# Every fourth weight unit: lo by a ScalarE copy and an accumulating DMA in place of a VectorE subtraction

## The chip, the cores and the metric

The kernel runs on one core of a Trainium2 chip. The time is device microseconds from launch to end. A profile is one execution recorded by the hardware profiler; its span goes from the first to the last instruction. Engines are called PE (TensorE, matmuls), PEld (its weight loads), DVE (VectorE), ACT (ScalarE), POOL (GpSimd) and SP (SyncE, which here only issues DMAs).

## The reference

A decoder trunk on 256 tokens of width 2048, float32, two layers. Layer 0 mixes tokens with an 8-head retention, layer 1 with sliding-window attention; each layer then has a SwiGLU of hidden width 5632 and a gated addition of a per-layer embedding. What matters here is that nearly all work is `h @ w` for large weights:

```
for i in range(DEPTH):
    h = rmsnorm(x, norm_mix[i])
    x = x + (retention_mixer(h, ret_w_in, ret_gn, ret_w_out) if i == 0
             else swa_mixer(h, swa_w_in, swa_sinks, swa_w_out))
    gate, up = split(rmsnorm(x, norm_ffn[i]) @ ffn_w_in[i], 2)
    x = x + (silu(gate) * up) @ ffn_w_out[i]
    x = x + sigmoid(rmsnorm(x, norm_ple[i]) @ ple_w_gate[i]) * (p[i] @ ple_w_proj[i])
return rmsnorm(x, norm_final)
```

The weights are read once each, 494 MB in all from HBM.

## The kernel before

TensorE multiplies in a shorter float32 form, float32r. To keep precision, every operand is split exactly into two parts: hi is the value rounded to float32r, lo is what is left over. A product is three matmuls: activation hi times weight hi (line 159), activation hi times weight lo (line 160), activation lo times weight hi (line 161).

The weights come in **units**: 256 rows by 512 columns, laid out as 128 partitions by 2 by 512, so 512 KB and one run of 4 KB in each partition. Eight units or more, over the whole contraction, make a **chunk**: 512 output columns for all 256 tokens, accumulated in two PSUM tiles. A unit takes 2 row blocks x 2 token tiles x 3 products = 12 matmuls. There are 928 units: 256 in the retention, 264 in each SwiGLU (8 a chunk going in, 22 a chunk going out), 36 in each embedding stage, 72 in attention.

`run` goes through all units in one order. At the step of unit i it issues the load of unit i + 5 (`LOADS`; SP, line 130, into one of five raw buffers), then the split of unit i + 3 (`AHEAD`; `split_weights`, into one of four hi and four lo buffers), then the twelve matmuls of unit i. With the last unit of a chunk its accumulators are evicted (`done`), and what follows from them (transposes on VectorE, splits of the new activations, scores, softmax) is put into `side`, a list of generators that are advanced by one step behind each unit. Each engine carries out its instructions in this program order, and a semaphore holds an instruction back until its operands are there and its target buffer is free.

The split of a weight unit is line 208, a ScalarE copy of raw into hi with rounding, and line 209, a VectorE subtraction raw - hi into lo. The raw buffer is free when both have read it; hi and lo are free when the unit's last matmuls have read them.

POOL computes only a few powers for the norms (lines 265, 360, 702) after its start.

Of the kernel before, what the change touches and what calls it, by code (L numbers as in the profile page):

```python
# [15 lines left out]
ALU = mybir.AluOpType  # L16
# [27 lines left out]
class Lhs:  # L44
    """A transposed activation, split exactly into two float32r parts."""

# [8 lines left out]
class Chunk:  # L55
    """512 output columns for all tokens, accumulated over the whole contraction, in pieces of
    a token tile and some of the columns."""

# [6 lines left out]
class Unit:  # L65
    """KU blocks of 128 rows of a weight, in one chunk's columns."""

    def __init__(self, chunk, src, kts, lhs):
        self.chunk, self.src, self.kts, self.lhs = chunk, src, kts, lhs
        self.w = None  # L70


class Stage:
    """A part of the trunk with tiles of its own, from its first unit to its last."""

# [3 lines left out]
    def linear(self, w, block, lhs, done, units=None, chunk=None):  # L79
        """One chunk: block of 512 columns of a weight laid out by `_units`."""  # L80
        ch = chunk or Chunk(self, done)
        for u in units if units is not None else range(w.shape[1]):
            self.units.append(Unit(ch, w[block, u], range(KU * u, KU * u + KU), lhs))
            ch.left += 1
# [3 lines left out]
def tile_trunk(ctx, tc, ins, out):  # L88
# [18 lines left out]

    # ---------------------------------------------------------------- streams
    side = deque()
# [23 lines left out]
    def split_weights(u):  # L133
        raw = u.w
        hi = whi.tile([P, KU, NW], F32R, name="hi")
        lo = wlo.tile([P, KU, NW], F32R, name="lo")
        for part in u.parts:
            split(hi[:, part, :], lo[:, part, :], raw[:, part, :])
        u.w = (hi, lo)

    def multiply(u, which, left):
        """The unit's products for some pieces of its chunk; `left` of the chunk's units are
        still to come."""
        ch = u.chunk
        need(u.lhs, u.kts)
        if ch.acc is None:
            ch.acc = []
            for n, (_, cols) in enumerate(ch.pieces):
                bank, name = (ps_acc, "acc") if n < NT else (ps_at, "at")
                ch.acc.append(bank.tile([P, NW], F32, name=name)[:, : cols.stop - cols.start])  # L150
        hi, lo = u.w
        for j, k in enumerate(u.kts):
            first = not ch.begun and j == 0
            last = left == 0 and j == KU - 1
            for n in which:
                t, cols = ch.pieces[n]
                sl = slice(t * P, (t + 1) * P)
                xh, xl = u.lhs.hi[:, k, sl], u.lhs.lo[:, k, sl]
                nc.tensor.matmul(ch.acc[n], xh, hi[:, j, cols], start=first, stop=False)  # L159
                nc.tensor.matmul(ch.acc[n], xh, lo[:, j, cols], start=False, stop=False)  # L160
                nc.tensor.matmul(ch.acc[n], xl, hi[:, j, cols], start=False, stop=last)  # L161

    def run(stages, begin):
        """All units in order, their weights AHEAD units ahead; between them, steps of side work.
        The products of the units that end the last chunk go piece by piece of its output."""
        units = [(st, u) for st in stages for u in st.units]
        for n, (_, u) in enumerate(units[:LOADS]):
            if n < AHEAD:
                next(begin)
            load(u, 1 if n else KU)  # L170
            if n < AHEAD:
                split_weights(u)
        side.append(begin)
        now = None
        pools = ExitStack()
        last = [u for _, u in units[-AHEAD - 1 :]]
        assert len({id(u.chunk) for u in last}) == 1
        for i, (st, u) in enumerate(units):
            if st is not now:
                pools.close()  # L180
                st.open_(st, pools)
                now = st
            if i + LOADS < len(units):
                load(units[i + LOADS][1])
            if i + AHEAD < len(units):
                split_weights(units[i + AHEAD][1])
            if u is last[0]:
                break
            ch = u.chunk
            ch.left -= 1  # L190
            multiply(u, range(len(ch.pieces)), ch.left)
            ch.begun = True
            if ch.left == 0:
                g = ch.done(ch.acc)
                if g is not None:
                    side.append(g)
            step_side()
        ch = last[0].chunk
        for n, (t, cols) in enumerate(ch.pieces):
            for i, u in enumerate(last):  # L200
                multiply(u, [n], len(last) - 1 - i)
            ch.done(ch.acc[n], t, cols)
        pools.close()

    # ------------------------------------------------------------ small pieces
    def split(hi, lo, src, scale=None):
# [9 lines left out]
    def transpose_pair(srcs):  # L216
        """Two [128, 128] blocks of both token tiles -> a PSUM tile [128, 2, S]."""
        tr = ps_tr.tile([P, 2, S], F32, name="tr")
# [5 lines left out]
    def transposes(dst, src):  # L224
        """Steps that transpose src [128, NT, 512] into dst [128, 4, S], by blocks of 32 x 32."""
        n = P // SQ
# [10 lines left out]
    def blocks(src, i):  # L237
        """Blocks 2i and 2i + 1 of 128 columns of both token tiles."""
        return [[src(t)[:, b * P : (b + 1) * P] for t in range(NT)] for b in (2 * i, 2 * i + 1)]

    class Norm:
        """Sums of squares of the residual's chunks, and the transposed residual times the gain.
        The scale by token, inv, is applied behind the product with the weights."""

# [22 lines left out]
        def places(self, c, src):  # L267
            """Steps that put a chunk's four transposed blocks in place."""
            for j in range(4):
# [8 lines left out]
    def residual(stage, norm, c):  # L278
        """A chunk of an output projection onto the residual, then the next norm's part."""

# [14 lines left out]

    # --------------------------------------------------------------- retention
    def retention(norm, next_norm, w_in, w_out):
# [97 lines left out]

    # ---------------------------------------------------- sliding-window attention
    def swa(norm, next_norm, w_in, w_out):
# [36 lines left out]
        def q_done_of(j):  # L434
            def q_done(acc):
# [12 lines left out]
                def scores(i):  # L448
                    """Of heads 2i and 2i + 1: the numerators and denominators' parts."""
                    ats = [ps_at.tile([P, 3 * P], F32, name="at") for _ in range(2)]  # L450
# [97 lines left out]
        for j in range(SKV):  # L548
            stage.linear(w_in, j, norm.lhs, q_done_of(j))
        # The first chunks' last units wait for the last group of heads.  # L550
        n = KD // KU
# [7 lines left out]

    # --------------------------------------------------------------------- FFN  # L560
    def ffn(layer, norm, next_norm):
# [57 lines left out]

    # --------------------------------------------------------------------- PLE  # L620
    def ple(layer, norm, next_norm, final):
# [12 lines left out]
        def pair(c):  # L634
# [3 lines left out]
            def gate_done(acc):  # L638
# [7 lines left out]
                def later():  # L646
                    # The last reads of the old operand are queued: its place is free.
                    for b, xt in enumerate(st["xt"]):
# [35 lines left out]
            def gate_last(acc, t, cols):  # L684
                """A piece of the last chunk; with a token tile's last one, its rows go out."""
                fin, rest, row = st["fin"], st["rest"], xs[:, t, :]
# [37 lines left out]

    # ------------------------------------------------------------------- trunk
    norms = [Norm(w, layer) for layer in range(DEPTH) for w in range(3)] + [Norm(None, 0)]
# [14 lines left out]
    def load_x():  # L741
        """The first norm's operand comes transposed, in step with the first chunk's weights."""
        for b in range(KD // KU):
# [19 lines left out]
def _constants():  # L763
    """Tables that follow from the shapes alone."""
    h = np.arange(RH, dtype=np.float64)
# [14 lines left out]
def _units(w):  # L780
    """[K, N] -> [N / 512, K / 256, 128, 2, 512]: each unit in one piece, by partitions."""
    k, n = w.shape
# [3 lines left out]
def _heads(w):  # L786
    """The retention's columns by heads: q and k, v, g."""
    q, k, v, g = np.split(w, [RH * RK, 2 * RH * RK, 2 * RH * RK + RH * RV], axis=1)
# [46 lines left out]
```

## Time and profile before

| | |
|---|---|
| time, median of 2 runs | 2649.66 us (2649.51 to 2649.82) |
| span of the profiled execution | 2647.9 us |
| runs less the span | 1.6 to 1.9 us |
| PE, PEld busy | 2629.2, 2142.7 us |
| DVE, ACT, POOL busy | 1817.2, 1223.7, 14.6 us |
| DMA | 497.79 MB, 188 GB/s |

The profiled execution's own time isn't given apart from its span; the runs lie 1.6 to 1.9 us above that.

How to read the lines: a group of instructions gives line, engine, operation, target<-sources, shapes and count, then busy time, the mean duration in ns of one, and after a second bar the idle time of the engine just before them with what ended it. A line of waits reads "who <- for whom: us in total, times, longest us". A line of the time line is start, duration, engine, line, operation, and in brackets the idle time before it and who ended it. A line of DMA issues ends with KB each and the median time from issue to landing. The chain of work is followed backwards from the last instruction, at each step to what released it.

### The profile page before, as it was taken

The page shows a single profiled execution, that of the slowest core. Times are in us where ns is not written, and L with a number is a line of the kernel's source. Part 1 is how long each engine was busy: PE and PEld are TensorE (multiplying, and loading weights), DVE is VectorE, ACT ScalarE, POOL GpSimd, SP SyncE. Part 2 cuts the span into 40 slices and gives each one's busy share as a digit, 9 for nine tenths or more (in the row PEclk, how much of TensorE's full clock was granted, in tenths as well). Part 3 has the DMA queues.
Part 4 walks back from the last instruction along what each step waited for, and adds up shares of the span by engine and source line. Part 5 has one row for each costly group of instructions (what it writes and reads, how often), then busy time and mean ns, then how long its engine had stood idle before and what let it go on. Part 6 is the DMA issues. An engine that isn't in the chain of part 4 may idle for free.

```text
span 2647.9 us, 31279 instructions
## 1 busy us (share of the span) xinstructions
PE 2629.2 (99%) x11632; PEld 2142.7 (81%) x11632; DVE 1817.2 (69%) x2567; ACT 1223.7 (46%) x1527; POOL 14.6 (1%) x30
## 2 busy tenths in 40 slices
PE   8999999999999999999999999999999999999998
PEld 6888888888888888888888887777888888888887
DVE  6777777766666667676555786888757575755565
ACT  6444444444444444444444555555444444444444
POOL 0000000000000000000000000000000000000000
PEclk9999999999999999999999999999999999999999
DMA  8555555565566565656655655346666666555564
GB/s 277 185 185 186 185 186 183 181 190 184 194 192 193 191 197 190 198 186 197 190 187 187 190 193 169 121 135 202 189 198 189 197 194 194 192 188 187 189 207 144
DMA packets 140506, 497.79 MB, mean 188 GB/s; under 512 B 15809, under 2 KB 19009, under 8 KB 140225
## 3 DMA queue, kind: packets, MB, share of 16 engines
q1 hardware_dynamic: 140064, 495.73, 58.5%
q8 instruction: 91, 1.49, 0.2%
q14 instruction: 63, 0.51, 0.1%
q10 hardware_dynamic: 288, 0.07, 0.0%
HBM read 493.63 MB, written 2.10 MB: 187 GB/s over the span
## 4 chain that ended last, share of the span: by engine, by line
PE 95%; DVE 3%; issue 1%; DMA 1%; ACT 0%; SPq 0%; ACTq 0%; POOLq 0%; POOL 0%; DVEq 0%
PE acc L159 31%; PE acc L161 31%; PE acc L160 31%; DVE lo L209 1%; DVE xt L233 1%; PE at L454 1%; PE tr L506 0%; PE at L532 0%; DMA raw<-in_ret_w_in 0%; PE at L323 0%; DVE xTl L212 0%; DVE qkT L233 0%; DMA xs<-in_x 0%; PE at L350 0%; PE at L352 0%
## 5 line engine op out<-in xcount | busy, mean ns | idle before, releaser
L209 DVE TENSOR_TENSOR lo<-raw,hi 128x1024 fp32r<-128x1024 f32 (+1 forms) x929 | 1131.8, 1221 | 720.2 <-ACT hi L208 712.8
L208 ACT ACTIVATE hi<-raw 128x1024 fp32r<-128x1024 f32 (+1 forms) x929 | 982.0, 1058 | 1210.9 <-PE acc L161 1117.4
L159 PE MATMUL acc<-hi,xTh 128*128 128x512 f32 x2592 | 1011.0, 390 | 6.6 <-ACT hi L208 5.4
L161 PE MATMUL acc<-hi,xTl 128*128 128x512 f32 x2592 | 1008.0, 389 | 0.8 <-DVE xTl L212 0.6
L160 PE MATMUL acc<-lo,xTh 128*128 128x512 f32 x2592 | 1008.7, 389 | 0.0
L159 PEld LDWEIGHTS acc<-hi,xTh 128*128 128x128 f32 x2592 | 487.3, 188 | 111.6 <-ACT hi L208 5.6
L161 PEld LDWEIGHTS acc<-hi,xTl 128*128 128x128 f32 x2592 | 487.0, 188 | 103.6 <-DVE xTl L212 2.5
L160 PEld LDWEIGHTS acc<-lo,xTh 128*128 128x128 f32 x2592 | 487.3, 188 | 100.5 <-issue 0.7
L161 PE MATMUL acc<-hi,hTl 128*128 128x512 f32 x704 | 278.4, 396 | 0.0
L160 PE MATMUL acc<-lo,hTh 128*128 128x512 f32 x704 | 278.4, 395 | 0.0
L159 PE MATMUL acc<-hi,hTh 128*128 128x512 f32 x704 | 278.4, 395 | 0.0
L233 DVE STREAM_TRANSPOSE xt<-h 32x256 f32<-32x256 f32 x352 | 153.6, 436 | 6.8
L161 PEld LDWEIGHTS acc<-hi,hTl 128*128 128x128 f32 x704 | 132.2, 188 | 32.1
L160 PEld LDWEIGHTS acc<-lo,hTh 128*128 128x128 f32 x704 | 132.2, 188 | 32.1
L159 PEld LDWEIGHTS acc<-hi,hTh 128*128 128x128 f32 x704 | 132.2, 188 | 31.9
L233 DVE STREAM_TRANSPOSE xt<-xs 32x256 f32<-32x256 f32 x320 | 139.5, 436 | 6.0
L161 PE MATMUL acc<-hi,yTl 128*128 128x512 f32 x256 | 101.2, 396 | 0.0
L160 PE MATMUL acc<-lo,yTh 128*128 128x512 f32 x256 | 101.2, 395 | 0.0
L159 PE MATMUL acc<-hi,yTh 128*128 128x512 f32 x256 | 101.2, 395 | 0.0
L233 DVE STREAM_TRANSPOSE qkT<-qk 32x256 f32<-32x256 f32 x128 | 55.8, 436 | 10.2 <-ACT qk L315 8.1
L211 ACT ACTIVATE xTh<-xt,gains 128x256 fp32r<-128x256 f32 x80 | 35.8, 499 | 56.0 <-DVE xt L233 51.6
L159 PEld LDWEIGHTS acc<-hi,yTh 128*128 128x128 f32 x256 | 48.1, 188 | 11.7
(124 smaller groups left out, 1178.2 us busy)
## 6 DMA issues: line engine op xcount, KB each, us to landing
raw<-in_ffn_w_in SPq DMA_DIRECT2D x352, 512.0 KB, 4.2
raw<-in_ret_w_in SPq DMA_DIRECT2D x191, 512.0 KB, 3.6
raw<-in_ffn_w_out SPq DMA_DIRECT2D x176, 512.0 KB, 4.0
raw<-in_ret_w_out SPq DMA_DIRECT2D x64, 512.0 KB, 4.0
raw<-in_ple_w_gate SPq DMA_DIRECT2D x64, 512.0 KB, 3.8
raw<-in_swa_w_in SPq DMA_DIRECT2D x40, 512.0 KB, 3.7
raw<-in_swa_w_out SPq DMA_DIRECT2D x32, 512.0 KB, 3.7
raw<-in_ple_w_proj SPq DMA_DIRECT2D x8, 512.0 KB, 4.0
```

Source lines behind the costliest of these rows:

```text
L159: nc.tensor.matmul(ch.acc[n], xh, hi[:, j, cols], start=first, stop=False)
L160: nc.tensor.matmul(ch.acc[n], xh, lo[:, j, cols], start=False, stop=False)
L161: nc.tensor.matmul(ch.acc[n], xl, hi[:, j, cols], start=False, stop=last)
L208: nc.scalar.activation(hi, src, AF.Copy)
L209: nc.vector.tensor_tensor(lo, src, hi.bitcast(F32), op=ALU.subtract)
L211: nc.scalar.activation(hi, src, AF.Copy, scale=scale)
L233: nc.vector.transpose(dst[b * SQ : (b + 1) * SQ, :, :, a, :], src[a * SQ : (a + 1) * SQ, :, :, b, :])
L454: nc.tensor.matmul(ats[e][:, 0:P] if b == 0 else ats[e][:, P : 3 * P], qT[sl, i, b * P : (b + 1) * P], kT[sl, j, 0 : (b + 1) * P], start=True,
```

## The change

For units `units[3:-4]`, counted from 0, every one with n % 4 == 1 is marked. In `split_weights` a marked unit is no longer split by lines 208 and 209 part by part. ScalarE first writes minus the rounded raw into lo; then POOL issues a DMA that adds the raw weights onto lo in place; then ScalarE writes hi as before. In alternation the DMA's source is the raw tile in SBUF (n % 8 == 1) or once more the weight in HBM (n % 8 == 5). -hi + raw equals raw - hi, so lo is the same number. VectorE has no part in a marked unit.

```diff
 class Unit:
     def __init__(self, chunk, src, kts, lhs):
         self.chunk, self.src, self.kts, self.lhs = chunk, src, kts, lhs
         self.w = None
+        self.summed = None
...
     def split_weights(u):
         raw = u.w
         hi = whi.tile([P, KU, NW], F32R, name="hi")
         lo = wlo.tile([P, KU, NW], F32R, name="lo")
-        for part in u.parts:
-            split(hi[:, part, :], lo[:, part, :], raw[:, part, :])
+        if u.summed is not None:
+
+            nc.scalar.activation(lo, raw, AF.Copy, scale=-1.0)
+            nc.gpsimd.dma_start(lo, raw if u.summed else u.src, accum_op=ALU.add)
+            nc.scalar.activation(hi, raw, AF.Copy)
+        else:
+            for part in u.parts:
+                split(hi[:, part, :], lo[:, part, :], raw[:, part, :])
         u.w = (hi, lo)
...
     def run(stages, begin):
         units = [(st, u) for st in stages for u in st.units]
+        for n, (_, u) in enumerate(units[AHEAD : -AHEAD - 1]):
+            if n % 4 == 1:
+                u.summed = n % 8 == 1
```

The rest of the diff takes comments and docstrings out.

## The prediction

> **What bounds the kernel now.** I read the page's busy times first, then the chain that ended last, then who waited for whom, then the time line of a quiet stretch.
>
> ```profile
> span 2647.9 us, 31279 instructions
> PE 2629.2 (99%) x11632; PEld 2142.7 (81%) x11632; DVE 1817.2 (69%) x2567; ACT 1223.7 (46%) x1527; POOL 14.6 (1%) x30
> PEclk9999999999999999999999999999999999999999
> PE 95%; DVE 3%; issue 1%; DMA 1%; ACT 0%; SPq 0%; ACTq 0%; POOLq 0%; POOL 0%; DVEq 0%
> PE acc L159 31%; PE acc L161 31%; PE acc L160 31%; DVE lo L209 1%; DVE xt L233 1%; PE at L454 1%; PE tr L506 0%; PE at L532 0%; DMA raw<-in_ret_w_in 0%; PE at L323 0%; DVE xTl L212 0%; DVE qkT L233 0%; DMA xs<-in_x 0%; PE at L350 0%; PE at L352 0%
> ```
>
> TensorE is busy for 2629.2 of 2647.9 us with the granted clock in the top tenth throughout, and 95% of the chain is its matmuls. A busy PE need not be PE at its peak, so the time line has to show whether the products follow each other at a fixed step:
>
> ```profile
> 999.77 0.39 PE L160 MATMUL acc<-lo,xTh 128*128 128x512 f32 x1
> 1000.00 0.39 PE L161 MATMUL acc<-hi,xTl 128*128 128x512 f32 x1
> 1000.22 0.39 PE L159 MATMUL acc<-hi,xTh 128*128 128x512 f32 x1
> 1000.42 1.06 ACT L208 ACTIVATE hi<-raw 128x1024 fp32r<-128x1024 f32 x1 [1.66 <-PE acc L161]
> 1001.51 1.23 DVE L209 TENSOR_TENSOR lo<-raw,hi 128x1024 fp32r<-128x1024 f32 x1 [1.49 <-ACT hi L208]
> ...
> 1008.38 0.39 PE L159 MATMUL acc<-hi,xTh 128*128 128x512 f32 x1
> ...
> 1008.61 0.39 PE L160 MATMUL acc<-lo,xTh 128*128 128x512 f32 x1
> ```
>
> Starts are 0.22 to 0.23 us apart; twelve make a unit of 2.72 us, and three units lie between 1000.22 and 1008.38. Nothing on VectorE is in this sequence. So at most 18.7 us (2647.9 less 2629.2) are to be had from any help to another engine, 0.7%. The ends of waits say the same:
>
> ```profile
> ACT hi L208 <- PE acc L161: 1117.4, 673, 3.1
> DVE lo L209 <- ACT hi L208: 712.8, 517, 3.3
> PE acc L159 <- ACT hi L208: 5.4, 1, 5.4
> SPq L130 <- DVE lo L209: 2115.2, 890, 8.8
> ```
>
> ScalarE waits for TensorE to give up a hi buffer, VectorE waits for ScalarE, and SP waits for VectorE to give up a raw buffer: each runs as far ahead as its buffers let it. TensorE's one long wait is 5.4 us at the start.
>
> **The change part by part.** Of 928 units, `units[3:-4]` are 921; n % 4 == 1 takes 230 of them, 115 with raw as the source (n % 8 == 1) and 115 with the weight in HBM.
>
> ```profile
> L209 DVE TENSOR_TENSOR lo<-raw,hi 128x1024 fp32r<-128x1024 f32 x927 | 1130.5, 1222 | 718.7 <-ACT hi L208 711.4
> L208 ACT ACTIVATE hi<-raw 128x1024 fp32r<-128x1024 f32 x927 | 980.8, 1059 | 1209.4 <-PE acc L161 1117.4 <-issue 64.3 <-ACT hi L208 10.3
> ```
>
> Removed: 230 VectorE subtractions of 1.222 us, 281 us, so VectorE goes from 1817 to some 1536 us. VectorE's lo is 1% of the chain, so under 1.5% or 40 us; a quarter of that is 10 us. I take nothing for it, with 10 us below as a bound, because the two stages where it shows (attention and its output) also get the new wait.
>
> Added on ScalarE: 230 copies of 1.059 us, 244 us, from 1224 to 1467 us of 2648. In the quiet stretch ScalarE stood idle 1.66 us of each 2.72 us, so the extra copy fits before the next hi is due. In program order lo comes first, then hi; hi moves back by 1.06 us, and since it started 8 us before its use (1000.42 against 1008.38), it is not late. Queued behind are the next hi and the evictions, which have accumulators to spare; in the attention stages with 72 units, 18 of them chosen, the worst is 18 x 1.06 = 19 us against at most 18 x 1.22 = 22 us given back on VectorE. I take zero.
>
> Added on POOL: 230 DMA issues. After its start POOL has nothing else but powers, the 16 of this row and eight in the norms.
>
> ```profile
> L360 POOL TENSOR_TENSOR rs<-ve,mhalf 128x1 f32<-128x1 f32 x16 | 8.6, 540 | 506.6 <-DVE ve L358 506.6
> ```
>
> Each issue waits for its ScalarE copy; a power behind it comes late by an issue or two, and its product (`on`, L362) is used only a chunk of eight units later. Nothing is taken for it.
>
> Added on the path: the **latency of the accumulating DMA**. This is the term that decides. The copy to lo can start when the L160 product at 999.77 has ended, at 1000.16, and would end at 1000.16 + 1.06 = 1001.22. The data must have landed at 1008.61. So the allowance from the end of the copy to the landing is **7.4 us**. Of such a DMA the trace shows nothing, so its latency L is bounded by the nearest transfers:
>
> ```profile
> DMA to landing us min/median/max: 3.0/4.0/7.9
> raw<-in_ffn_w_in SPq DMA_DIRECT2D x352, 512.0 KB, 4.2
> raw<-in_ret_w_in SPq DMA_DIRECT2D x191, 512.0 KB, 3.6
> out<-xs SPq DMA_DIRECT2D x8, 256.0 KB, 2.5
> fin<-in_norm_final SPq DMA_DIRECT2D x1, 1024.0 KB, 5.8
> ```
>
> From below, L is an ordinary 512 KB load, 4.0 us, plus 0.54 us for POOL to do an instruction in software: 4.5 us, hidden everywhere. From above it is the slowest load of the run, 7.9 us, plus 0.54: 8.4 us. Between them I take the row it is nearest to by bytes: an accumulation reads the source and the old lo, 1 MB for 512 KB written, as `fin` reads 1 MB in 5.8 us. With 0.54 us on POOL and 0.1 us for the wait that is **6.4 us**, an estimate, hidden by 1.0 us in the quiet stretch.
>
> It is not hidden where ScalarE is behind. In the retention stage, once a head, a chosen unit's copy stands behind the split of y:
>
> ```profile
> 164.76 0.89 ACT L211 ACTIVATE yTh<-xt,gn 128x256 fp32r<-128x256 f32 x2
> 165.56 2.21 ACT L208 ACTIVATE hi<-raw 128x1024 fp32r<-128x1024 f32 x2
> ...
> 172.12 0.39 PE L160 MATMUL acc<-lo,xTh 128*128 128x512 f32 x1
> ```
>
> There the copy would end at 165.56 + 1.06 = 166.62 and lo is due at 172.12: 5.5 us, so 0.9 us late. Eight heads have this place, and I allow as many at the boundaries of the other stages: 16 x 0.9 = 14 us.
>
> The raw buffer is held longer for the 115 units that read it by DMA: until 1.06 + 6.4 = 7.5 us after the copy begins, not some 2.3 us (1000.42 to 1002.74). The next load into it lands about 4.3 us later, 11.8 us, and its unit is split five units later, 13.6 us. That is hidden by 1.8 us, and would be late from L = 8.2 on.
>
> DMA engines:
>
> ```profile
> q1 hardware_dynamic: 140064, 495.73, 58.5%
> HBM read 493.63 MB, written 2.10 MB: 187 GB/s over the span
> ```
>
> 58.5% of 2647.9 us for 495.73 MB is 3.125 us a MB, so 1.64 us of all 16 engines for a load of 0.524 MB. Four units last 2647.9 / 232 = 11.41 us and need 6.55; 4.86 us are left for one accumulation. At one load's price (1.64) the share becomes 73%, at two (3.28) 87%; both fit.
>
> The Trainium skill, in "Collectives: The Full Stack", section "The bandwidth ceiling: the fold count and why AG ≠ RS ≠ AR", says that a DMA that adds needs two source reads through one read ring, so that it runs at half a copy's rate, the adding itself costing nothing. By that rule the share is the 87% above and the sum stays. The same skill in "DMA: Bandwidth & Descriptors", section "Anatomy of one DMA — SWDGE (gpsimd) path", gives some 2.0 us plus bytes over 436 GB/s for a DMA issued from POOL; an estimate by that page is 3.2 us for 512 KB and 4.4 us with the second read. No row here shows such a DMA; the ordinary 512 KB loads took 4.0 us. By the page the sum would be 2650 us with no late place at all.
>
> Sum on the profiled execution: 2647.9 + 14 = 2662 us of span. The runs shown, 2649.51 to 2649.82, are 1.6 to 1.9 us above that span; with 1.8 us, **2664 us**.
>
> **The rivals.**
>
> *Hidden, a little late in places* (the forecast): 2664 us, chance 0.48. For it speaks the `fin` row; against it, that the margin of 1.0 us is thinner than the spread of ordinary loads (3.0 to 7.9 us).
>
> *The accumulation lands late in every fourth unit* (the other side): TensorE waits in front of the first L160 product of each chosen unit. The wait isn't recovered, because the copy of the next chosen unit starts only when TensorE releases a buffer, so each microsecond beyond 7.4 costs 230 us. It decides from L = 7.6 us on (0.23 us x 230 = 53 us, 2%). At the upper bound of 8.4 us it is 1.0 x 230 = 230 us, and 16 x 1.9 = 30 us for the tight places: 2664 - 14 + 260 = 2910 us. For it speaks that the accumulation starts together with loads on the same engines, and the largest landing; against it, that those landings belong to the few crowded stretches. Chance 0.34.
>
> *The DMA engines become the bound.* If adding costs the engines as much as four loads (6.55 us), four units need 13.1 us, not 11.41: 230 x 1.69 = 389 us, 3039 us. For it: the engines are at 58.5% before. Against: 4.86 us are free, three loads' worth. Chance 0.10.
>
> *It doesn't do what it says*: the accumulation is cut into short pieces, so that it is one DMA by name and many small ones by cost. The price is that of the two cases above or more, at least 2910 us. No row speaks for it; a unit's row in a partition is one run of 4 KB in both source and target. Chance 0.06.
>
> *VectorE's relief counts.* 10 us of chain, at the utmost 18.7 us: 2631 to 2640 us. Even that is inside 2%. For it: attention's output stage, where L209 ended waits of TensorE. Chance 0.02.
>
> **How the numbers follow.** The likeliest case gives 2664. The range runs from 2640 (2650 less VectorE's 10 us) to 2930 (the upper bound of the latency, 2910, with 20 us for the attention stages' ScalarE). It leaves out most of the last three cases, 0.18. Within 2% is about what a measurement of this kernel can tell from no change; the forecast and the relief lie there, 0.50 less a little for the first's upper end and more for the milder half of the second: 0.50. Faster by over 2% would need 53 us where 18.7 are to be had: 0.01. The rest, 0.49, is slower.
>
> **What would show it.** In the changed kernel's profile: L209 with some 697 full-size executions and VectorE near 1536 us; ScalarE near 1467 us; a new POOL queue with 230 issues and their time to landing, right if 6.4 us or less, wrong from 7.4 on; the DMA share between 73% and 87%. If late landing wins, PE's products of L160 will wait for a DMA some 230 times, the chain will have a DMA share of 5% or more, and the units after 1000 us will be more than 2.72 us apart in every fourth case. If the engines are the bound, the DMA row stands at nines and loads land late too, so that hi is waited for as well. What makes the forecast wrong above all is the latency estimate: it rests on one row of another kind of transfer.

## The result, and the profile after

2853.68 us, median of two runs (2847.16 to 2860.21), against 2649.66: ratio 1.0767, 95% interval 1.0749 to 1.0785. The profiled execution's span is 2858.4 us, 210.5 more than before.

The changed kernel's page, with the same parts as before. Lines moved: 159 to 161 are now 166 to 168, 208 and 209 are 218 and 219; the new lines are 140 (copy to lo), 141 (the DMA) and 142 (hi).

```profile
span 2858.4 us, 31750 instructions
PE 2682.6 (94%) x11632; PEld 2153.0 (75%) x11632; DVE 1547.0 (54%) x2337; ACT 1440.8 (50%) x1757; POOL 215.3 (8%) x260
...
q1 hardware_dynamic: 140064, 495.73, 51.3%
q0 software_dynamic: 33120, 120.60, 23.9%
...
PE 60%; DMA 31%; ACT 4%; issue 2%; DVE 1%; POOL 0%; SPq 0%; ACTq 0%; POOLq 0%
```

VectorE and ScalarE came out as worked out (1547 for 1536, 1441 for 1467 us). But the chain, 95% TensorE before, is now 31% DMA. The DMA issues of the same page say which:

```profile
lo<-raw POOLq DMA_DIRECT2D x115, 512.0 KB, 4.6
lo<-in_ffn_w_in POOLq DMA_DIRECT2D x44, 512.0 KB, 8.9
lo<-in_ret_w_in POOLq DMA_DIRECT2D x23, 512.0 KB, 8.6
lo<-in_ffn_w_out POOLq DMA_DIRECT2D x22, 512.0 KB, 9.1
```

The same addition lands in 4.6 us when its source is raw in SBUF, and in 8.6 to 9.1 us when it is the weight in HBM. Who waited for whom, in the changed kernel:

```profile
PEld acc L167 <- DMA lo<-in_ffn_w_in: 88.2, 44, 2.9
PE acc L167 <- DMA lo<-in_ffn_w_in: 69.6, 43, 2.5
```

All 44 units of that weight with HBM as the source make TensorE's weight loads wait, and 43 its products. Nothing of this size stands there for raw. One of them in the time line of the changed kernel, and the raw-sourced unit after it (start, duration, engine; SP's rows are the ordinary loads, and most rows between are left out):

```profile
1004.14 0.33 SPq L131 DMA_DIRECT2D raw<-in_ffn_w_in  x1
1004.24 1.06 ACT L140 ACTIVATE lo<-raw 128x1024 fp32r<-128x1024 f32 x1 [1.38 <-PE acc L167]
1005.59 0.88 POOL L141 DMA_DIRECT2D lo<-in_ffn_w_in  x1 [10.01 <-ACT lo L140]
1006.27 0.33 SPq L131 DMA_DIRECT2D raw<-in_ffn_w_in  x1
1009.58 0.33 SPq L131 DMA_DIRECT2D raw<-in_ffn_w_in  x1
1012.25 0.33 SPq L131 DMA_DIRECT2D raw<-in_ffn_w_in  x1
1012.42 0.39 PE L166 MATMUL acc<-hi,xTh 128*128 128x512 f32 x1
1013.86 0.50 PE L167 MATMUL acc<-lo,xTh 128*128 128x512 f32 x1 [1.05 <-DMA lo<-in_ffn_w_in]
...
1015.54 0.33 SPq L131 DMA_DIRECT2D raw<-in_ffn_w_in  x1
1016.46 1.06 ACT L140 ACTIVATE lo<-raw 128x1024 fp32r<-128x1024 f32 x1 [2.20 <-PE acc L167]
1017.81 0.87 POOL L141 DMA_DIRECT2D lo<-raw  x1 [11.34 <-ACT lo L140]
...
1022.42 0.81 SPq L131 DMA_DIRECT2D raw<-in_ffn_w_in  x2
```

The L167 product was due at 1012.65 and started at 1013.86. The load of 1004.14 was under way when the HBM-sourced addition was issued, and three more were issued before it landed (1006.27, 1009.58, 1012.25). Between 1015.54 and 1022.42 there was none: the raw-sourced addition holds its raw buffer, and SP, which issues in order, stands still until it has landed. SP's waits in the changed kernel:

```profile
SPq L131 <- DMA lo<-raw: 836.2, 114, 12.7
```

So two things differ between the two kinds: the source, and the loads that run beside. Counted over the whole trace from the issues and landings, a raw-sourced addition found 0.9 ordinary loads in flight at its issue and 0.03 more were issued before it landed (means); an HBM-sourced one found 1.8, and 2.9 more were issued.

What the lateness costs: the copy ends at 1005.30 and POOL starts 0.29 us later; 0.29 + 8.9 - 7.4 (the allowance) = 1.8 us late by the median, times 115 is 207 us, an estimate, near the loss.

The trace divides the loss otherwise. TensorE's idle time rose by 157 us (from 18.7 to 175.8); its products waited 159.2 us in 100 waits for an addition. Its busy time rose by 53 us (from 2629.2 to 2682.6). Half of that is a slower clock at some of the waits. One place, first its products, then a stretch of it (from and to, length, busy time and count of PE, PEld, DVE, ACT and POOL, granted clock, DMA share, GB/s):

```profile
190.24 0.50 PE L167 MATMUL acc<-lo,xTh 128*128 128x512 f32 x1 [1.94 <-DMA lo<-in_ret_w_in]
...
192.25 0.63 PE L167 MATMUL acc<-lo,xTh 128*128 128x512 f32 x1
192.67 0.63 PE L168 MATMUL acc<-hi,xTl 128*128 128x512 f32 x1
```
```profile
191.20:194.40 3.20, 3.20 (x10) 2.42 (x9) 3.09 (x8) 0.21 (x1) 0.00 (x0) 0.50 0.50 179
```

The products follow each other at 0.43 us there, not 0.23. The changed kernel's trace has 16 such stretches at a granted clock of 0.50, 15 of 3.4 us and one of 6.8; the kernel before has none while it multiplies. The 133 products in them, 0.20 us longer each, are 27 us. Each stretch begins during a wait of 1.78 us or more or within 1.4 us of its end; 33 other waits as long brought none, and what decides isn't shown. The other half of the 53 us lies at the waits themselves: the product before a wait runs out alone (0.16 us) and the one behind it is 0.11 us slow (1013.86 to 1014.20), an estimate of 100 x 0.27 = 27 us.

### The profile page after: what moved, and what is told of

Its sections match the earlier page's. It is cut to its first block, busy times and chain, and to the rows that moved or that the text cites. A ratio compares the mean times of both kernels' runs of the same rounds, so it can differ in the third digit from the quotient of the medians.

```text
span 2858.4 us, 31750 instructions
## 1 busy us (share of the span) xinstructions
PE 2682.6 (94%) x11632; PEld 2153.0 (75%) x11632; DVE 1547.0 (54%) x2337; ACT 1440.8 (50%) x1757; POOL 215.3 (8%) x260
## 3 DMA queue, kind: packets, MB, share of 16 engines
q1 hardware_dynamic: 140064, 495.73, 51.3%
q0 software_dynamic: 33120, 120.60, 23.9%
## 4 chain that ended last, share of the span: by engine, by line
PE 60%; DMA 31%; ACT 4%; issue 2%; DVE 1%; POOL 0%; SPq 0%; ACTq 0%; POOLq 0%
PE acc L167 21%; PE acc L168 19%; PE acc L166 19%; DMA lo<-in_ffn_w_in 13%; DMA lo<-in_ret_w_in 6%; DMA lo<-in_ffn_w_out 6%; ACT lo L140 4%; DMA lo<-in_ple_w_gate 2%; DMA lo<-in_ret_w_out 2%; DMA lo<-in_swa_w_out 1%; DMA lo<-raw 1%; PE at L464 0%; DMA raw<-in_ret_w_in 0%; PE at L542 0%; PE tr L516 0%
## 5 line engine op out<-in xcount | busy, mean ns | idle before, releaser
L219 DVE TENSOR_TENSOR lo<-raw,hi 128x1024 fp32r<-128x1024 f32 (+1 forms) x699 | 852.9, 1220 | 1134.5 <-ACT hi L218 1131.5
L218 ACT ACTIVATE hi<-raw 128x1024 fp32r<-128x1024 f32 (+1 forms) x699 | 739.0, 1057 | 835.7 <-PE acc L168 738.3
L167 PE MATMUL acc<-lo,xTh 128*128 128x512 f32 x2592 | 1024.7, 395 | 114.4 <-DMA lo<-in_ffn_w_in 69.6
L167 PEld LDWEIGHTS acc<-lo,xTh 128*128 128x128 f32 x2592 | 491.4, 190 | 247.3 <-DMA lo<-in_ffn_w_in 88.2
L140 ACT ACTIVATE lo<-raw 128x1024 fp32r<-128x1024 f32 x230 | 243.8, 1060 | 441.7 <-PE acc L167 441.1
L167 PE MATMUL acc<-lo,hTh 128*128 128x512 f32 x704 | 282.8, 402 | 30.1 <-DMA lo<-in_ffn_w_out 30.1
L142 ACT ACTIVATE hi<-raw 128x1024 fp32r<-128x1024 f32 x230 | 239.7, 1042 | 5.9 <-PE acc L168 3.8
L141 POOL DMA_DIRECT2D lo<-raw x115 | 99.7, 867 | 1378.2 <-ACT lo L140 1343.4
L167 PEld LDWEIGHTS acc<-lo,hTh 128*128 128x128 f32 x704 | 133.9, 190 | 70.0 <-DMA lo<-in_ffn_w_out 38.4
L167 PE MATMUL acc<-lo,yTh 128*128 128x512 f32 x256 | 103.2, 403 | 10.3 <-DMA lo<-in_ret_w_out 10.3
```

The source lines that it names most:

```text
L140: nc.scalar.activation(lo, raw, AF.Copy, scale=-1.0)
L141: nc.gpsimd.dma_start(lo, raw if u.summed else u.src, accum_op=ALU.add)
L142: nc.scalar.activation(hi, raw, AF.Copy)
L218: nc.scalar.activation(hi, src, AF.Copy)
L219: nc.vector.tensor_tensor(lo, src, hi.bitcast(F32), op=ALU.subtract)
```

## The experiments

Each is a change to the changed kernel; "before" was run beside each.

| run | time, us | ratio to before (95%) | landing on lo, min/median/max us |
|---|---|---|---|
| changed kernel | 2853.68 | 1.0767 (1.0749 to 1.0785) | 4.5/6.9/9.8 (both kinds) |
| 1: all raw | 2688.98 | 1.0144 (1.0127 to 1.016) | 4.5/6.0/9.0 |
| 2: all HBM | 2839.99 | 1.0717 (1.0685 to 1.0749) | 5.6/7.5/9.9 |
| 3: all HBM, raw held | 2808.35 | 1.0598 (1.0576 to 1.0619) | 5.3/7.6/10.0 |
| 4: all from a fixed SBUF tile | 2762.77 | 1.0426 (1.0405 to 1.0446) | 4.8/6.8/9.9 |
| 5: 115 raw only | 2659.54 | 1.0035 (1.0019 to 1.0051) | 4.6/5.4/8.8 |
| 6: 115 HBM only | 2840.36 | 1.0717 (1.0686 to 1.0749) | 5.6/8.3/9.7 |
| 7: all HBM, one unit earlier | 2662.78 | 1.0049 (1.0026 to 1.0072) | 5.2/7.0/9.5 |
| 8: all HBM, copy without adding | 2710.84 | one run | 3.8/6.9/8.3 |
| 9: all HBM, half loads | 2692.24 | 1.016 (1.0139 to 1.018) | 5.4/6.4/9.6 |
| 10: raw, one unit earlier | 2685.98 | 1.0132 (1.0117 to 1.0147) | 4.5/5.1/9.1 |
| 11: the same near attention only | 2654.95 | 1.002 (1.0011 to 1.003) | 4.5/6.0/7.3 |
| 12: buffers of 7, 10, 11, no marks | 2653.12 | 1.0013 (1.0003 to 1.0022) | |

**Which half makes the loss.** Runs 1, 2, 5 and 6 change only the marks.

```diff
-                u.summed = n % 8 == 1
+                u.summed = True        # run 1;  run 2: False
```
```diff
-            if n % 4 == 1:
+            if n % 8 == 1:             # run 5, source raw;  run 6: n % 8 == 5, source HBM
```

Run 1, all from raw:

> All 230 marked units take raw in SBUF as the source, none the weight in HBM. Theory A (the loss comes only from the 115 units whose source is HBM, landing 8.6 to 9.1 us after the issue; those from raw land in 4.6 us and are hidden by 2.5 us): within 5 us of the kernel before, 2645 to 2655 us, no wait of TensorE for a DMA onto lo. Rival R (the extra ScalarE copies, the POOL issues or the fuller DMA engines cost time by themselves): 2700 us or more.

Run 5, the 115 raw-sourced units alone:

> Only the 115 units with raw as the source are marked (n % 8 == 1); the other 115 are split on VectorE as before. Theory A (raw-sourced accumulations are hidden): 2650 to 2665 us. Rival R (copies, issues and DMA load cost by themselves): half of what all 230 cost, 2669 us or more.

Run 6, the 115 HBM-sourced units alone:

> Only the 115 units with the weight in HBM as the source are marked (n % 8 == 5). Theory A (these alone make the loss): the changed kernel's time again, about 2850 us. Theory P (an HBM-sourced accumulation is slow, and a raw-sourced unit before it makes it slower, because it holds back loads that then run beside the next accumulation): landing about 7.5 us as in the run with 230 HBM units, not 8.9, and half of that run's loss, 2650 + 190 / 2 = 2745 us.

The HBM units alone cost 190 us (2840 less 2650), the raw units alone 10; together 200, and the changed kernel lost 204. So theory A holds in runs 5 and 6, and theory P, that the raw-sourced neighbour does the damage, falls by the time, though the landing came down from 8.9 to 8.3. The rival R of copies, issues and a fuller DMA falls with run 5: of its 10 us, TensorE's products waited 8.2 for an addition. Run 1 missed A's 5 us: 39 us are lost. Where, run 1's waits and time line show:

```profile
PEld acc L167 <- DMA lo<-raw: 49.3, 46, 5.5
...
176.61 1.04 ACT L140 ACTIVATE lo<-raw 128x1024 fp32r<-128x1024 f32 x1
...
185.66 0.50 PE L167 MATMUL acc<-lo,xTh 128*128 128x512 f32 x1 [0.73 <-DMA lo<-raw]
```

46 of 230 are late. The one shown is the place once a head at which ScalarE is behind; the product before it started at 184.54, so it is 0.9 us late beyond the step of 0.23 us. With all from raw a landing takes 6.0 us, not 4.6. The loads held off are made up between the additions: by the trace 2.4 were in flight when an addition was issued, against 0.9 in the changed kernel (and 1.5 in run 5, where it landed in 5.4).

Run 2:

> All 230 marked units take the weight in HBM. Theory A: each is late by (2858 - 2648) / 115 = 1.83 us, so 2650 + 230 x 1.83 = 3070 us. Rival B (an HBM unit is late only because the raw-sourced unit before it held back loads, which then bunch up): without raw-sourced units the waits go, 2700 us or less.

2840 us fits neither: twice as many units lose the same in all, 0.83 us each instead of 1.65 in run 6, and land in 7.5 instead of 8.3 us. Why a denser row of them lands sooner isn't settled: the loads beside are nearly as many (1.1 in flight at the issue and 2.7 issued before the landing, against 1.3 and 2.9 in run 6).

**Source, loads or adding.** Run 3 puts this behind the DMA, so that raw isn't free until it has landed:

```diff
+            held = small.tile([P, 1], F32, name="held")
+            nc.gpsimd.tensor_tensor(held, lo[:, 0, 0:1].bitcast(F32), raw[:, 0, 0:1], op=ALU.add)
```

> All 230 marked units take the weight in HBM, but a one-column POOL instruction that reads lo and raw is put behind each accumulating DMA, so that the raw buffer isn't free, and the next load isn't issued, before the accumulation has landed. Theory C (an accumulation is slow when loads run beside it on the same engines): it lands in 4.6 to 5.5 us, and the time is 2650 to 2700 us. Theory S (adding from HBM is slow by itself): it lands in 8 us or more, and the time is 3070 us or more.

Landing stayed at 7.6 us, time 2808: inconclusive. Holding did not clear the engines. SP stood still for 1629.9 us in 229 waits for the new instruction; 7.1 us of standstill a time leaves loads in arrears, which then follow each other closely and run into the next addition: 3.1 were in flight when it was issued, against 1.1 in run 2, though hardly any (0.04) were issued before it landed. Ordinary loads of the big input weight land in 5.1 us, against 4.5 in run 2.

```profile
SPq L131 <- POOL held L144: 1629.9, 229, 9.7
raw<-in_ffn_w_in SPq DMA_DIRECT2D x352, 512.0 KB, 5.1
```

Run 4 takes the source from a tile in SBUF that nothing waits for (the embedding's operand, one run of 4 KB a partition), so that raw is free at once as in run 2 and only the source differs:

```diff
-            nc.gpsimd.dma_start(lo, raw if u.summed else u.src, accum_op=ALU.add)
+            nc.gpsimd.dma_start(lo, still, accum_op=ALU.add)
```

> All 230 accumulations read a constant 4 KB-a-row tile in SBUF (so lo is wrong) in place of raw, so that raw is free as soon as ScalarE has read it and the loads run beside the accumulation. Theory C: it lands in 8 us or more though its source is SBUF, and the time is about 3000 us. Theory S: it lands in 4.6 to 5.5 us, and the time is 2650 us.

Neither theory alone. 113 us are lost, between run 1's 39 (SBUF, loads held off) and run 2's 190 (HBM, loads beside); landing 6.8, between 6.0 and 7.5. Of run 2's 190 us, some 77 go with the source (190 - 113), some 74 with loads that are no longer held off (113 - 39). The loads beside were nearly the same in runs 4 and 2 (1.2 and 1.1 in flight, 2.3 and 2.7 issued before the landing), so the source is worth about 0.7 us of landing there, a sixth of the 4.3 us between the two kinds in the changed kernel.

Run 9 changes the loads and leaves the additions:

```diff
...
+        if half:   # from the 41st load on
+            nc.sync.dma_start(raw[:, 0, :], u.src[:, 0, :])
+            raw = raw[:, 0:1, :].to_broadcast([P, KU, NW])
...
```

> As the run with all 230 units from HBM, but from the 41st unit on each ordinary load moves only the first half of its weights (256 KB in place of 512 KB; the split reads that half twice, so hi and lo are wrong there). The accumulating DMAs are whole. Theory C (the loads beside an accumulation on the same engines make it late): landing falls from 7.5 to 6.5 us or less, time 2650 to 2700 us. Theory S (source HBM and adding alone): landing stays at 7 us or more, time about 2840 us.

Run 9's DMA queues and landing on lo:

```profile
q1 hardware_dynamic: 140064, 262.94, 30.8%
q0 software_dynamic: 33120, 120.60, 28.0%
DMA to landing us min/median/max: 5.4/6.4/9.6
```

Half the loads' bytes, and the loss falls from 190 to 42 us. Theory C's mechanism holds: the loads beside the addition make it late. Whether they do so on the DMA engines or in HBM, run 9 can't tell, since it halves both; run 4's additions, which read no HBM, were late too.

Run 8 leaves out the adding:

```diff
-            nc.gpsimd.dma_start(lo, raw if u.summed else u.src, accum_op=ALU.add)
+            nc.gpsimd.dma_start(lo, u.src)
```

> All 230 marked units with the weight in HBM as the source, but the DMA from POOL only copies and doesn't add (so lo is the whole weight). Theory C (adding doubles the time of a packet on the DMA engines): packets as in an ordinary load, landing 5 to 6 us, 2650 to 2700 us. Rival Q (it is the DMA from POOL, or the second read of HBM, that is slow): landing 7 us or more, 2800 us or more.

2711 us in its one run, landing 6.9, so between the two. The queue's own row (packets, MB, share of 16 engines), run 8 first, then run 2:

```profile
span 2709.0 us, 31746 instructions
q0 software_dynamic: 33120, 120.60, 15.6%
```
```profile
span 2831.0 us, 31746 instructions
q0 software_dynamic: 33120, 120.60, 26.6%
```

15.6% of 2709 us for 120.6 MB is 3.5 us a MB, 26.6% of 2831 us is 6.2: adding takes 1.8 times the engine time of copying the same bytes. Yet it adds only 0.6 us to the median landing, and half of that is POOL, which was busy 215.2 us in run 2 and 138.0 in run 8, 0.34 us less for each of the 230 issues. The loss triples because 7.4 us is a threshold: from the end of the copy, 154 of run 2's additions landed later than that, and 96 of run 8's.

**Is it only latency?** Run 7 gives the copy and the DMA one unit more of lead, with five lo buffers and four raw ones:

```diff
+    def sum_lo(u):
+        if u.summed is not None:
+            u.lo = wlo.tile([P, KU, NW], F32R, name="lo")
+            nc.scalar.activation(u.lo, u.w, AF.Copy, scale=-1.0)
+            nc.gpsimd.dma_start(u.lo, u.src, accum_op=ALU.add)
...
+            if i + AHEAD + 1 < len(units):
+                sum_lo(units[i + AHEAD + 1][1])
             if i + AHEAD < len(units):
                 split_weights(units[i + AHEAD][1])
```

> All 230 marked units read HBM, but the copy to lo and the accumulating DMA are put one unit earlier and ahead of that step's split, with five lo buffers and four raw buffers. Theory L (the whole loss is latency beyond the lead of three units): the allowance grows from 7.4 to some 10 us or more, and the time is 2650 to 2690 us though the landing stays at 7 to 9 us. Rival D (the DMA engines are short of throughput): 2800 us or more.

All 230 units read HBM, landing is still 7.0 us, and 2662.78 us is 0.5% from before. Run 7's landing and chain:

```profile
DMA to landing us min/median/max: 5.2/7.0/9.5
PE 94%; DMA 3%; DVE 1%; issue 1%; ACT 1%; SPq 0%; ACTq 0%; POOLq 0%; POOL 0%; DVEq 0%
```

Theory L holds in the main: all but 13 of the 190 us are gone, and TensorE's products wait only 7.0 us for an addition. But run 7's additions also land a little sooner than run 2's (7.0 against 7.5 us); why isn't settled. Summed over the additions, what lies beyond 7.4 us between the end of the copy and the landing is 152 us in run 2 (190 were lost), 72 in run 4 (113), 43 in run 8 (61), 27 in runs 1 and 9 (39 and 42). In run 7 it is 83 us, and 13 were lost. So the lead does most of it, and the sooner landing, 83 in place of 152, a part. The DMA engines have the throughput.

**A version that beats both?** Run 10 is run 7 with raw as the source, marks from unit 28; run 11 the same with only the 22 marks in and beside attention; run 12 has no marks.

> All marked units from unit 28 on take raw as the source, and copy to lo and DMA come one unit earlier (five lo buffers, four raw buffers). Theory L: the 39 us that raw-sourced units lost in 230 go, 2645 to 2655 us. That TensorE leaves at most 18.7 us to be had, of which some 10 at the start, puts the floor at 2640 us. Rival: the four raw buffers or the held raw make loads late, 2665 us or more.

> The same, but only the 22 marked units in and beside the attention stage, where VectorE ended waits of TensorE before. Relief: 3 to 8 us less than the kernel before, 2642 to 2647 us. Rival (no gain, since the extra ScalarE copy stands in the same chains): 2648 to 2655 us.

> No unit is marked; only the buffers are those of the runs with the longer lead (five lo, four raw). A control for the two runs before: 2649 to 2652 us if four raw buffers suffice, more if not.

No. Run 12 shows that these buffers cost 3 us by themselves; run 11 is 2 us above it, and their intervals overlap, so the relief that was expected of it didn't come. Run 10 missed its expectation too and is the rival's case: held raw buffers, now four, make loads late. Its copies to lo wait for loads longer than those of run 7, which holds no raw buffer (run 10 first, then run 7):

```profile
ACT lo L137 <- DMA raw<-in_ffn_w_in: 308.5, 77, 6.0
```
```profile
ACT lo L137 <- DMA raw<-in_ffn_w_in: 140.1, 74, 3.9
```

In run 10's chain both kinds of DMA have a share of their own:

```profile
PE acc L170 22%; PE acc L169 22%; PE acc L171 22%; DMA lo<-raw 12%; DMA raw<-in_ffn_w_in 7%; DVE xt L248 2%; DVE lo L224 2%; ACT hi L223 1%; PE at L469 1%; DMA raw<-in_ple_w_gate 1%; DMA xs<-in_x 1%; PE at L547 0%; PE tr L521 0%; DMA raw<-in_ffn_w_out 0%; PE at L338 0%
```

## Why the prediction was wrong, point by point

- **The bound.** Right. TensorE sets the time; 281 us of VectorE's work taken away brought nothing, as runs 5 and 11 show too. No version fell below 2650 us.
- **The allowance of 7.4 us.** Right, and the number on which all turns: run 7 raised it and nearly all of the loss went, though by its own landings 83 us of lateness would have been left at 7.4.
- **The latency of 6.4 us.** This is the step that failed. It was one value for two kinds of addition, taken from a 1 MB load. Raw-sourced ones took 4.6 us plus 0.29 from the end of the copy to POOL's start, 4.9, below it; HBM-sourced ones 8.9 plus 0.29, 9.2 us, above even the upper end of 8.4. The 0.1 us taken for that wait stood in no row. The upper end was the slowest single load plus POOL's 0.54 us; an addition from HBM with 1.8 loads in flight at its issue and 2.9 issued before it landed is slower than that as a median. The sharing was named in the rival (the accumulation "starts together with loads on the same engines") and not priced.
- **The held raw buffer.** The working asked only whether the next load would come late. It did not see the other side: while raw is held SP issues no loads, and so a raw-sourced addition has fewer of them beside it. Not held off (run 4), an addition from SBUF lands in 6.8 us. The half that seemed burdened is the half that was hidden.
- **The price of lateness.** The rival's mechanism happened, with 115 units in place of 230 and 1.8 us each in place of 1.0. The two errors nearly cancel: it gave 2910 us, measured were 2854, and that nearness is luck. It also counted waits alone; 27 us of the loss are the halved clock that came with some of them.
- **The DMA engines as a bound.** Right that they are not one: 51.3% and 23.9% of the span, 75%, inside the forecast 73% to 87%, and run 7. The Trainium skill, in "Collectives: The Full Stack", section "The bandwidth ceiling: the fold count and why AG ≠ RS ≠ AR", has the adding step of a ring collective at half the rate of the copying one, because of its second source read; 1.8 times in runs 8 and 2 agrees roughly. The estimate by the Trainium skill's page "DMA: Bandwidth & Descriptors", section "Anatomy of one DMA — SWDGE (gpsimd) path", 4.4 us with the second read, agrees with the 4.5 us of the quickest raw-sourced landing and with no HBM-sourced one (5.2 us at the least).
- **Tight places.** Right in kind: in run 1 the place once a head is late, in the row above by 0.9 us. That this is the 0.9 worked out is luck: the copy there ends at 177.65 for a product due at 184.77, an allowance of 7.1 us in place of 5.5, and the data came after 8.0 us in place of 6.4. Too few: 46 waits in place of 16.

## What to carry to other kernels

Where TensorE is busy 99% of the span, as here, moving work from one helper engine to another has little to win (18.7 us at the most) and much to lose; what decided here is whether the new path is longer than the lead in buffers. Price a DMA's latency with the traffic that its own issue time brings: which buffer its instructions free, and which transfers that lets start beside it. Here the DMA that held the next load's buffer landed sooner, and paid for it in late loads where the buffers were four (run 10). And look at the busy time as well as at the waits: a quarter of this loss was not waiting.

## What the runs showed of the hardware

An accumulating DMA of 512 KB landed in 4.5 us at the least from SBUF (changed kernel and run 1) and in 5.2 us at the least from HBM (run 7). Adding took 1.8 times the engine time of a copy of the same bytes (6.2 against 3.5 us a MB on 16 engines). Issuing such a DMA kept POOL for 0.87 us; without adding (run 8) it was 0.53. With ordinary loads beside it, the median landing from HBM was 7.5 us (run 2), 8.3 (run 6) and 8.9 (the big input weight in the changed kernel). Of TensorE's 49 waits of 1.78 us or more in the changed kernel, 16 came with a stretch of 3.4 us, once 6.8, at a granted clock of 0.50.
